# P V products of a head pair in one visit, the relative bias as one float32r pass, and another set of stream delays

## The chip, the cores and the metric

The kernel runs on one core of one Trainium2 chip. The metric is the device time of one execution in microseconds; the time given is the median of several runs. The engines are TensorE (PE, with its weight loads as PEld), VectorE (DVE), ScalarE (ACT), GpSimd (POOL) and SyncE (SP, which here only issues DMAs).

## The reference

One decoder layer on 512 tokens of width 1024. Eight attention heads and eight Gated DeltaNet heads, all of width 64, share one input projection and one output projection; RMSNorms stand ahead of and behind both halves, and a squared-ReLU MLP of width 4096 follows.

```python
h = rms_norm(x, pre_mix_norm[l])
proj = einsum('bsd,dc->bsc', h, w_in[l])
att_q, att_k, att_v, gdn_qkv, gdn_z, gdn_a, gdn_b = split(proj, split_points, axis=-1)
o_att = moba_attention(att_q, att_k, att_v, rel_bias)
o_gdn = gated_deltanet(gdn_qkv, gdn_z, gdn_a, gdn_b, conv_w[l], A_log[l], dt_bias[l], gdn_norm_w[l])
mix = einsum('bsc,cd->bsd', concatenate([o_att, o_gdn], axis=-1), w_out[l])
x = x + rms_norm(mix, post_mix_norm[l])
h = rms_norm(x, pre_mlp_norm[l])
m = einsum('bsf,fd->bsd', square(relu(einsum('bsd,df->bsf', h, w_up[l]))), w_down[l])
x = x + rms_norm(m, post_mlp_norm[l])
```

The attention works on blocks of 256 keys and picks three past blocks for each query. With 512 tokens there are two blocks, so it is plain causal attention. Its logits are `q k / 8 + rel_bias[head, bucket(q_pos - k_pos)]` with 32 buckets of distance; then softmax, then the product with `v` (P V below). The DeltaNet part runs over chunks of 64 tokens: a convolution of four taps with SiLU, normalized q and k, the inverse of a unit lower triangular matrix per chunk and head, and a recurrence over eight chunks.

## The kernel before

Large products are made from float32r operands split into a high part `hi` and a remainder `lo`; `mm3` issues the three products hi hi, hi lo and lo hi. ACT rounds to `hi`, and DVE or POOL subtracts to get `lo` (`split`, `load_split`, `ended`). Transposes and small products stay in float32; in the trace a float32 product of 128x64 shape leaves two records.

**Order of TensorE.** TensorE's instructions run in the order in which the Python program emits them. The program is a set of generators (streams) that a small planner, `Weave` (L47), interleaves. It keeps a clock `now` that `mm` (L96) and `transpose` (L100) advance by an assumed duration. A stream yields a delay, or the name of a mark; the planner runs the stream of lowest rank whose time has come. Delays come from the table `WAIT` (L20) by kind; `SINGLE` (L22) overrides the n-th use of a kind, for example `('conv_k', 1)`. `RANK` (L24) gives the order of the streams, `LEAD` (L25) a priority that the other engines' scheduler uses, `START` (L28) some fixed moments of the opening, and `LO_DVE` (L30) the range of weight loads whose `lo` is subtracted on DVE rather than POOL. A delay is thus not a wait on the chip: it decides where in TensorE's queue the next piece of a stream stands. On the chip TensorE waits if the data of its next instruction aren't there. ACT, DVE and POOL run in emission order in the opening (`pre_norm`, `in_order`) and in the scheduler's order afterwards, until the MLP. SP issues DMAs.

**The streams.**

- `projections` (the main stream, rank 5 and last): 24 items of 128 output columns in the sequence of `ORDER` (L29), each 24 matmuls of 512 columns, and the attention's `v` by token. `x0` to `x3` are the q's and `y0` to `y3` the k's of the four pairs of attention heads. `x2` and `x3` wait for the marks `att0` and `att1`, whose buffers they take.
- `take_k`, `take_q`, `take_v`, `take_z`: convolution and so on of each DeltaNet item as it leaves PSUM; `conv_k` is the delay between an item's convolution and the transposes of `kraw`.
- `chunks`, `inverse`, `scan`, `finish_o`: DeltaNet. The inverse is 31 steps of two DVE instructions; the scan's matmuls have 32*32, 64*64 and 128*64 shapes.
- `bias`, `scores`, `values`: the attention. Four pairs of heads, four blocks of 128 tokens.
- `weights_out`, `output`, `weights_up`, `up0`: output projection and the start of the MLP, which runs behind all this in an order of its own.

**PSUM.** Eight banks in three tags: `mm` (2), `g` (3) and `a` (3), by `bank` (L175).

**Bias.** `bias_in` (L197) loads a 33 x 640 table of zeros and ones (`c_hot`, as `hot`) and the 32 x 8 biases with a 33rd row of -1e30 (`rb`), right behind the loads of `x` and of the first weights. `bias` (L651) multiplies them in float32 in two products of 512 and 128 columns and stores the result to DRAM (`d_e`), from which `scores` reads it in a skewed form.

**Scores and values.** For each pair `scores` (L682) makes rows 3, 2, 1 and 0 of the logits, the triangular part alone, and their exponentials; each row sets a mark `row{p}{q}` after the delay `rows`. `values` (L720) transposes the exponentials (`block(k)`: keys of block k, all later queries, into bank tag `a`, copied by ACT into `ph` tiles, of which four stand) and multiplies with `v` (`product(k, P)`: one matmul for each of the two heads, onto one bank `po`, also of tag `a`). The order is

```python
P = block(3)
po = bank("a")
for k in (2, 1, 0):
    yield f"row{p}{k}"
    if k > 0:
        N = block(k)
    yield wait["pv"]
    product(k + 1, P)
    if k == 0:
        N = block(0)
    P = N
```

so the products of blocks 3, 2 and 1 come each after the delay `pv`, and the transposes of block 0 directly behind product 1. Then the mark `turned{p}` lets the next pair's scores begin; the reciprocal sums are transposed into a bank `rb`, ACT copies them to SBUF, and after the delay `pv0` the last product is issued. DVE multiplies `po` with the sums (`mx`), `split` rounds it, and `att{p}` is marked after the delay `att`.

Of the kernel before, what the change touches and what calls it, by code (L numbers as in the profile page):

```python
# [85 lines left out]
def layer(ctx, tc, nc, x, w_in, w_v, w_ab, w_out, w_up, w_down, conv_w, a_log, dt_bias, gdn_norm_w, rel_bias,  # L86
# [633 lines left out]
    def values():  # L720
        for p in range(4):
# [812 lines left out]
```

## Time and profile before

| | us |
|---|---|
| median of 3 runs | 635.08 |
| lowest and highest run | 632.75, 635.93 |
| span of the profiled execution, first to last instruction | 634.2 |

The profile gives the span of the profiled execution; a time of its own is not listed for it. The span is 0.88 us under the median of the runs. Mean granted TensorE clock: 0.998.

Busy time by stage, from the view by windows:

| us from the start | PE | DVE | ACT | POOL | DMA share |
|---|---|---|---|---|---|
| 0 to 20 | 17.47 | 9.55 | 10.61 | 9.20 | 0.66 |
| 120 to 140 | 20.00 | 18.80 | 9.09 | 2.59 | 0.27 |
| 140 to 160 | 19.70 | 18.72 | 8.24 | 0.00 | 0.28 |
| 180 to 200 | 19.75 | 6.06 | 16.38 | 7.72 | 0.17 |
| 240 to 260 | 19.60 | 10.61 | 15.44 | 3.99 | 0.31 |
| 360 to 634 (MLP) | 267.66 of 274 | 222.86 | 164.30 | 40.24 | 0.86 |

How to read it: a row of the views in order of time has the start in us, the time from the start to the end of the group, the engine, the line of the kernel, the operation, `out<-in` by the program's names, the tile shape of TensorE (contraction rows * output rows), the operand and the count of records; idle time ahead of it and what ended that stand in brackets. Matmuls are pipelined and their ends are modelled, so the distance between two starts says more than a duration.

### The profile page before, as it was taken

What the parts mean: (1) busy time and instruction counts of PE and PEld (TensorE: products, weight loads), DVE (VectorE), ACT (ScalarE), POOL (GpSimd) and SP (SyncE); (2) the same over time, 40 slices, a digit from 0 to 9 for tenths busy, and PEclk for the clock granted to TensorE, in tenths of its full rate; (3) what the DMA queues carried; (4) which work ended last, traced back from release to release, by engine and by line L of the source; (5) the groups of instructions that cost most, each with busy time, mean ns of one, the idle gap of its engine ahead of it and who ended that gap; (6) DMA issues with size and microseconds to landing.
All of it is one profiled execution on the core that took longest, in us unless ns stands there. A gap on an engine that the chain in (4) does not pass through costs nothing.

```text
span 634.2 us, 11129 instructions
## 1 busy us (share of the span) xinstructions
PE 622.9 (98%) x4359; PEld 524.1 (83%) x4359; DVE 443.7 (70%) x635; ACT 359.4 (57%) x610; POOL 157.9 (25%) x197
## 2 busy tenths in 40 slices
PE   8999999999999999999999999999999999999995
PEld 6877777877876777688998999999998888888884
DVE  4456667599724464658665678878789888887776
ACT  6366586254387548654225586566765656665661
POOL 4346555500234343004212311111130320000001
PEclk9999999999999999999999999999999999999999
DMA  7222332422731112563488899999999999867503
GB/s 247 78 90 83 84 109 76 128 88 71 186 94 52 36 35 82 188 229 132 162 336 233 159 276 268 228 241 286 270 264 340 310 291 285 270 213 283 198 1 132
DMA packets 60629, 113.16 MB, mean 178 GB/s; under 512 B 15734, under 2 KB 35321, under 8 KB 60194
## 3 DMA queue, kind: packets, MB, share of 16 engines
q1 hardware_dynamic: 42876, 83.09, 37.8%
q0 software_dynamic: 17696, 29.36, 22.2%
q8 instruction: 34, 0.56, 0.3%
q14 instruction: 17, 0.14, 0.1%
q10 hardware_dynamic: 6, 0.00, 0.0%
HBM read 106.65 MB, written 35.15 MB: 224 GB/s over the span
## 4 chain that ended last, share of the span: by engine, by line
PE 91%; DVE 3%; DMA 2%; ACT 2%; POOL 1%; issue 0%; POOLq 0%; DVEq 0%; SPq 0%; ACTq 0%
PE ps_mm L97 46%; PE ps_g L97 26%; PE ps_a L97 16%; PE ps_a L101 2%; PE ps_g L101 1%; DMA wo_raw<-in_w_out 1%; DMA xx<-in_x 1%; DVE conv L412 1%; DMA w_raw<-in_w_in 0%; DVE wo_l L143 0%; POOL w_lo L155 0%; POOL oss L192 0%; DVE hT_l L131 0%; POOL by L192 0%; DVE xs L249 0%
## 5 line engine op out<-in xcount | busy, mean ns | idle before, releaser
L130 ACT CAST wdh<-wd 128x1024 fp32r<-128x1024 f32 x53 | 55.9, 1054 | 51.4 <-PE ps_mm L97 22.6
L131 DVE TENSOR_TENSOR u_l<-w,u_h 128x1024 fp32r<-128x1024 f32 x46 | 56.2, 1224 | 37.3 <-ACT u_h L130 37.1
L131 DVE TENSOR_TENSOR wdl<-wd,wdh 128x1024 fp32r<-128x1024 f32 x53 | 64.9, 1224 | 22.2 <-ACT wdh L130 22.1
L130 ACT CAST u_h<-w 128x1024 fp32r<-128x1024 f32 x46 | 47.9, 1046 | 56.8 <-DVE w L1177 15.6
L97 PE MATMUL ps_mm<-hT_h,w_hi 128*128 128x512 f32 (+1 forms) x192 | 79.4, 413 | 0.0
L97 PE MATMUL ps_mm<-hT_l,w_hi 128*128 128x512 f32 (+1 forms) x192 | 74.6, 388 | 0.3 <-DVE hT_l L131 0.3
L97 PE MATMUL ps_mm<-hT_h,w_lo 128*128 128x512 f32 (+1 forms) x192 | 74.5, 388 | 0.0
L155 POOL TENSOR_TENSOR w_lo<-w_raw,w_hi 128x512 fp32r<-128x512 f32 x40 | 51.8, 1297 | 77.2 <-ACT w_hi L154 67.4
L1210 POOL DMA_DIRECT2D d_T<-in_w_down x32 | 33.0, 1033 | 143.8 <-DMA d_T<-in_w_down 82.4
L154 ACT CAST w_hi<-w_raw 128x512 fp32r<-128x512 f32 x56 | 34.6, 620 | 52.9 <-PE ps_mm L97 17.5
L97 PEld LDWEIGHTS ps_mm<-hT_h,w_hi 128*128 128x128 f32 x192 | 37.1, 193 | 11.3 <-issue 4.8
L97 PE MATMUL ps_mm<-wdh,u_h 128*128 128x512 f32 x116 | 45.2, 390 | 0.0
L97 PE MATMUL ps_mm<-wdl,u_h 128*128 128x512 f32 x116 | 45.1, 389 | 0.0
L97 PE MATMUL ps_mm<-wdh,u_l 128*128 128x512 f32 x116 | 45.1, 389 | 0.0
L97 PEld LDWEIGHTS ps_mm<-hT_h,w_lo 128*128 128x128 f32 x192 | 37.2, 194 | 7.5
L97 PEld LDWEIGHTS ps_mm<-hT_l,w_hi 128*128 128x128 f32 x192 | 37.3, 194 | 6.0 <-DVE hT_l L131 0.6
L412 DVE SCALAR_TENSOR_TENSOR conv<-ps_mm,cw,conv 128x511 f32<-128x511 f32 (+2 forms) x36 | 26.8, 745 | 11.3 <-ACT conv L409 11.0
L131 DVE TENSOR_TENSOR u_l<-f,u_h 128x1024 fp32r<-128x1024 f32 x28 | 34.1, 1217 | 0.0
L708 DVE CUSTOM_DVE_ANT_0 L<-ps_a,E 128x512 f32<-128x512 f32 (+3 forms) x32 | 14.4, 489 | 23.9 <-PE ps_a L97 23.7
L97 PE MATMUL ps_g<-wdh,u_h 128*128 128x512 f32 x80 | 31.1, 389 | 0.0
L97 PE MATMUL ps_g<-wdl,u_h 128*128 128x512 f32 x80 | 31.1, 389 | 0.0
L97 PE MATMUL ps_g<-wdh,u_l 128*128 128x512 f32 x80 | 31.1, 389 | 0.0
(452 smaller groups left out, 1761.3 us busy)
## 6 DMA issues: line engine op xcount, KB each, us to landing
d_T<-in_w_down POOLq DMA_DIRECT2D x48, 512.0 KB, 11.6
wd<-d_T SPq DMA_DIRECT2D x32, 512.0 KB, 6.2
w<-in_w_up SPq DMA_DIRECT2D x28, 512.0 KB, 8.0
wd<-in_w_down SPq DMA_DIRECT2D x24, 512.0 KB, 7.7
w_raw<-in_w_in SPq DMA_DIRECT2D x46, 256.0 KB, 2.7
wo_raw<-in_w_out SPq DMA_DIRECT2D x16, 256.0 KB, 3.4
d_T<-d_T POOLq DMA_DIRECT2D x8, 512.0 KB, 12.7
xx<-in_x SPq DMA_DIRECT2D x4, 512.0 KB, 6.4
```

The costliest lines, as they stand in the source:

```text
L97: nc.tensor.matmul(o, l, r, **kw)
L101: nc.tensor.transpose(o, i, ident[:k, :k])
L130: nc.scalar.copy(hi, src)
L131: tt(lo, src, f32(hi), op=OP.subtract)
L154: nc.scalar.copy(hi, raw)
L155: (sub or tt)(lo, raw, f32(hi), op=OP.subtract)
L412: stt(c[:, s:], p[:, :512 - s], cw[:, ft, j:j + 1], c[:, s:], op0=OP.mult, op1=OP.add)
L708: nc.vector.tensor_tensor_reduce(out=l, in0=s[hh][:, :w], in1=Es[hh][:, w - 1::-1], scale=1.0, scalar=3e38, op0=OP.add, op1=OP.min, accum_ ...
L1210: nc.gpsimd.dma_start(d_T[t][k], block(b, second)[k], accum_op=OP.add, max_dma_last_dim=1024)
```

## The change

Three parts.

1. `values` issues all four `block` transposes of a pair first and all eight P V matmuls (four `product` steps of two) together, after `rb` and the delay `pv0`. `po` is taken only then. The delay `pv` is no longer used. `ph` has eight buffers for four.
2. The bias product is made in float32r: the 33-row table is doubled to 97 rows (rows 0 to 32 and 64 to 96), the biases are split into a rounded part in rows 0 to 32 and the remainder in rows 64 to 96 of `rs`, and one pass multiplies both. New are a memset of `rs`, a copy of the table by POOL that rounds it to float32r, a copy by ACT and a subtraction by DVE; these three are issued at `START[3]`.
3. `WAIT`, `SINGLE`, `RANK`, `LEAD`, `START` and `LO_DVE` have other values, and in `ORDER` `v0` and `v1` change places. `SINGLE` has 147 entries where it had 36; among the new ones are `('pv0', 1): 4.83`, `('rows', 7): 8.76`, `('state', 5): 2.54` and `('scalars', 0): 4.42`, `('conv_k', 1)` stays 5.1 and `('kk_out', 0)` goes from 11.93 to 6.79.

```diff
-WAIT = {'h': 1.7, 'conv_k': 5.5, 'k': 5.19, 'conv_q': 6.15, 'q': 2.1, 'conv_v': 11.0, 'v': 6.02, 'z': 2.87, 'ab': 0.1, 'g': 11.93, 'scalars': 4.76, 'r_in': 0.65, 'r_out': 4.45, 'kk': 2.71, 'kk_out': 14.43, 'gl': 3.13, 'qk': 3.88, 'va': 0.83, 'a': 5.81, 'row': 1.38, 'rows': 5.12, 'pv': 1.54, 'att': 1.17, 'inverse': 1.23, 'merge': 11.0, 'p1': 2.8, 'p2': 1.7, 'w': 2.33, 'vn': 1.0, 'state': 1.21, 'o_in': 3.96, 'o': 3.73, 'wo': 0.97, 'wo_out': 17.6, 'normed3': 7.6, 'normed': 11.21, 'n': 1.7, 'up': 1.9, 'sums': 2.64, 'turned': 0.5, 'pv0': 1.53}
+WAIT = {'h': 0.86, 'conv_k': 5.48, 'k': 6.06, 'conv_q': 5.48, 'q': 2.49, 'conv_v': 11.04, 'v': 3.81, 'z': 2.47, 'ab': 2.97, 'g': 7.94, 'scalars': 6.37, 'r_in': 0.44, 'r_out': 4.15, 'kk': 3.12, 'kk_out': 21.2, 'gl': 5.7, 'qk': 2.04, 'va': 1.87, 'a': 5.44, 'row': 2.47, 'rows': 5.12, 'pv': 1.45, 'att': 3.93, 'inverse': 0.39, 'merge': 9.84, 'p1': 3.55, 'p2': 0.79, 'w': 1.67, 'vn': 1.0, 'state': 2.43, 'o_in': 3.89, 'o': 3.36, 'wo': 3.23, 'wo_out': 26.28, 'normed3': 11.89, 'normed': 13.4, 'n': 2.23, 'up': 0.86, 'sums': 2.41, 'turned': 0.42, 'pv0': 4.1}
...
-RANK = {'chunks': 1, 'inverse': 3, 'scan': 3, 'scores': 5, 'values': 5, 'finish_o': 2, 'take': 4}
-LEAD = {'chunks': 0, 'inverse': 100, 'scan': 100, 'scores': 0, 'values': 100, 'finish_o': 0, 'take': 200, 'take_a': 100}
+RANK = {'chunks': 2, 'inverse': 2, 'scan': 1, 'scores': 4, 'values': 4, 'finish_o': 3, 'take': 4}
+LEAD = {'chunks': 300, 'inverse': 50, 'scan': 200, 'scores': 100, 'values': 0, 'finish_o': 300, 'take': 50, 'take_a': 200}
...
-START = (5.5, 9.7, 18.5, 13.8, 30, 15.0)
-ORDER = "k0 q0 x0 k1 q1 q2 y0 k2 k3 z0 q3 x1 w0 v0 v1 v2 v3 y1 x2 y2 x3 y3 z1 z2 z3"
-LO_DVE = (26, 40)
+START = (6.58, 9.48, 15.98, 12.4, 30.84, 15.19)
+ORDER = "k0 q0 x0 k1 q1 q2 y0 k2 k3 z0 q3 x1 w0 v1 v0 v2 v3 y1 x2 y2 x3 y3 z1 z2 z3"
+LO_DVE = (29, 48)
...
     def bias_in():
-        hot, es = he[:33, :640], he[:8, 640:]
+        hot, es = he[:97, :640], he[:8, 640:]
...
+        rs = at.tile([97, 8], FR, name="rs", bufs=1)
+        nc.vector.memset(f32(rs), 0.0)
...
     def bias():
-        hot, es, rb = rel
+        hot, es, rb, rs = rel
+        hot_r = at.tile([128, 1280], FT, name="L")[:97, :640].bitcast(FR)
+        yield max(0, START[3] - weave.now)
+        nc.gpsimd.tensor_copy(hot_r, hot)
+        nc.scalar.copy(rs[:33], rb)
+        tt(rs[64:97], rb, f32(rs[:33]), op=OP.subtract)
         yield max(0, START[4] - weave.now)
         for a, b in ((0, 512), (512, 640)):
             pe = bank("a")
-            mm(pe[:8, :b - a], rb, hot[:, a:b], start=True, stop=True)
+            mm(pe[:8, :b - a], rs, hot_r[:, a:b], start=True, stop=True)
...
-                    pt = at.tile([128, 512], FT, name="ph", bufs=4)
+                    pt = at.tile([128, 512], FT, name="ph", bufs=8)
...
-            P = block(3)
-            po = bank("a")
+            P = {3: block(3)}
             for k in (2, 1, 0):
                 yield f"row{p}{k}"
-                if k > 0:
-                    N = block(k)
-                yield wait["pv"]
-                product(k + 1, P)
-                if k == 0:
-                    N = block(0)
-                P = N
+                P[k] = block(k)
             mark(f"turned{p}", wait["turned"])
             yield f"sums{p}"
             rb = bank("a")
...
             yield wait["pv0"]
-            product(0, P)
+            po = bank("a")
+            for k in (3, 2, 1, 0):
+                product(k, P[k])
...
-    hot = np.zeros((33, 640), f)
-    hot[bucket, 127 + d] = 1
-    hot[32, :127] = 1
+    hot = np.zeros((97, 640), f)
+    for o in (0, 64):
+        hot[o + bucket, 127 + d] = 1
+        hot[o + 32, :127] = 1
```

More of the change, by code (lines that the diff above doesn't have):

```diff
@@ L22 @@
-SINGLE = {('h', 0): 0.05, ('inverse', 6): 2.02, ('state', 6): 3.71, ('row', 5): 0.98, ('inverse', 18): 0.05, ('inverse', 25): 0.05, ('vn', 7): 0.05, ('pv', 2): 0.1, ('h', 1): 0.05, ('turned', 0): 0.9, ('conv_k', 0): 4.12, ('normed', 0): 10.21, ('wo', 1): 1.97, ('conv_q', 0): 8.0, ('inverse', 16): 1.63, ('state', 1): 1.57, ('row', 6): 0.38, ('conv_v', 1): 8.5, ('conv_q', 2): 7.0, ('conv_k', 1): 5.1, ('o_in', 1): 4.36, ('kk', 2): 2.03, ('h', 2): 0.85, ('rows', 2): 6.66, ('vn', 1): 0.75, ('pv', 4): 2.77, ('inverse', 0): 0.61, ('rows', 0): 5.52, ('pv', 6): 2.0, ('rows', 4): 0.1, ('conv_v', 0): 14.3, ('kk_out', 0): 11.93, ('gl', 0): 5.63, ('inverse', 27): 0.23, ('row', 12): 2.48, ('state', 0): 0.21}
@@ new lines @@
+SINGLE = {('h', 0): 4.85, ('inverse', 6): 2.02, ('state', 6): 3.66, ('row', 5): 0.98, ('inverse', 25): 0.05, ('vn', 7): 0.14, ('pv', 2): 0.1, ('normed', 0): 10.24, ('wo', 1): 0.05, ('conv_q', 0): 8.69, ('inverse', 16): 1.63, ('state', 1): 1.57, ('row', 6): 0.33, ('conv_v', 1): 7.83, ('conv_k', 1): 5.1, ('kk', 2): 2.03, ('vn', 1): 0.75, ('pv', 4): 2.77, ('inverse', 0): 0.93, ('rows', 0): 6.08, ('pv', 6): 2.0, ('rows', 4): 0.22, ('conv_v', 0): 14.23, ('kk_out', 0): 6.79, ('inverse', 27): 0.23, ('row', 12): 2.48, ('state', 0): 0.05, ('vn', 4): 0.05, ('g', 0): 11.27, ('pv0', 3): 5.63, ('n', 1): 2.8, ('row', 9): 4.41, ('inverse', 20): 1.09, ('state', 4): 1.35, ('inverse', 28): 4.43, ('rows', 7): 8.76, ('w', 2): 2.04, ('kk', 0): 2.54, ('normed3', 0): 7.79, ('n', 2): 1.44, ('o_in', 2): 4.99, ('state', 5): 2.54, ('r_in', 3): 1.7, ('w', 3): 2.33, ('scalars', 0): 4.42, ('rows', 5): 4.36, ('row', 3): 4.58, ('n', 0): 5.62, ('z', 3): 0.05, ('inverse', 3): 1.71, ('inverse', 9): 4.8, ('state', 2): 3.37, ('o_in', 1): 1.66, ('ab', 0): 1.85, ('inverse', 12): 1.27, ('va', 0): 0.05, ('o_in', 0): 0.94, ('sums', 0): 1.83, ('r_in', 0): 0.83, ('q', 3): 4.02, ('wo', 9): 2.75, ('rows', 11): 4.94, ('r_in', 2): 0.05, ('up', 1): 2.69, ('k', 0): 6.39, ('row', 13): 2.25, ('inverse', 21): 0.68, ('pv0', 2): 2.33, ('up', 6): 0.71, ('up', 2): 1.8, ('z', 1): 1.9, ('rows', 9): 5.32, ('rows', 6): 4.96, ('row', 15): 2.64, ('row', 1): 1.47, ('a', 0): 4.5, ('att', 2): 0.15, ('wo', 14): 10.37, ('wo', 13): 5.87, ('r_out', 2): 4.4, ('rows', 8): 4.94, ('v', 0): 13.69, ('conv_k', 3): 5.47, ('up', 0): 1.03, ('att', 1): 1.03, ('conv_q', 3): 4.72, ('normed', 1): 13.89, ('rows', 1): 6.91, ('inverse', 2): 0.05, ('wo', 8): 4.61, ('k', 1): 4.72, ('turned', 0): 0.05, ('vn', 3): 1.16, ('q', 2): 4.06, ('pv0', 1): 4.83, ('q', 0): 2.14, ('o', 1): 0.14, ('o', 3): 4.07, ('vn', 2): 3.12, ('k', 3): 5.87, ('up', 5): 2.84, ('wo_out', 0): 19.88, ('inverse', 10): 0.9, ('merge', 0): 10.94, ('v', 2): 12.67, ('w', 0): 1.68, ('inverse', 19): 1.66, ('pv0', 0): 4.87, ('conv_q', 1): 4.99, ('wo', 2): 1.79, ('z', 0): 0.05, ('inverse', 24): 1.39, ('a', 3): 5.23, ('wo', 11): 3.51, ('rows', 3): 6.28, ('inverse', 14): 0.15, ('att', 0): 3.37, ('row', 10): 2.37, ('conv_k', 0): 5.11, ('v', 3): 14.1, ('normed', 2): 12.25, ('z', 2): 0.05, ('row', 2): 2.64, ('kk', 1): 3.86, ('wo', 12): 3.29, ('r_in', 1): 0.05, ('turned', 3): 0.69, ('q', 1): 2.97, ('att', 3): 4.49, ('turned', 2): 0.25, ('v', 1): 8.52, ('up', 3): 0.37, ('wo', 4): 3.7, ('gl', 0): 5.22, ('kk', 3): 4.48, ('vn', 6): 1.14, ('sums', 1): 1.59, ('inverse', 4): 0.32, ('row', 8): 1.29, ('k', 2): 5.51, ('h', 1): 2.26, ('row', 14): 2.55, ('n', 3): 1.82, ('inverse', 1): 0.05, ('wo', 5): 6.26, ('p2', 0): 0.05, ('r_out', 1): 5.83}
@@ L203, in bias_in @@
         nc.sync.dma_start(rb[:32], rel_bias)
-        return hot, es, rb
+        rs = at.tile([97, 8], FR, name="rs", bufs=1)
+        nc.vector.memset(f32(rs), 0.0)
+        return hot, es, rb, rs
     def pre_norm(ahead):
```

## The prediction

> **What bounds the kernel now.** I read the page first: engine shares, the 40 slices, the chain that ended last.
>
> ```profile
> span 634.2 us, 11129 instructions
> ...
> PE 622.9 (98%) x4359; PEld 524.1 (83%) x4359; DVE 443.7 (70%) x635; ACT 359.4 (57%) x610; POOL 157.9 (25%) x197
> ...
> PE   8999999999999999999999999999999999999995
> ...
> PE 91%; DVE 3%; DMA 2%; ACT 2%; POOL 1%; issue 0%; POOLq 0%; DVEq 0%; SPq 0%; ACTq 0%
> ```
>
> TensorE is busy in every slice and is 91% of the chain. So a microsecond is won only if TensorE issues less, or if one of its own gaps closes; what other engines gain is worth nothing by itself. A busy PE isn't a full PE, however, since ends are modelled. I therefore go by starts, and ask next for the waits of PE in the first 280 us, the part that the change touches:
>
> ```profile
> PE ps_g L101 <- DVE kraw L416: 1.0, 1, 1.0
> ...
> PE ps_a L101 <- ACT ph L736: 0.3, 1, 0.3
> PE ps_a L97 <- ACT t L762: 0.2, 1, 0.2
> ```
>
> Little is left to win there: the largest wait behind the opening is 1.0 us, and the next that matter are on tiles of the bank tag `a`. The remainder has to come from how matmuls of different shapes follow each other. The order in time shows that:
>
> ```profile
> 132.28 0.39 PE L97 MATMUL ps_mm<-hT_h,w_lo 128*128 128x512 f32 x1
> 132.51 0.82 PE L101 MATMUL ps_a<-ident,L 128*128 128x128 f32 x6
> 133.09 0.48 PE L97 MATMUL ps_mm<-hT_h,w_hi 128*128 128x512 f32 x1
> 133.40 0.40 PE L97 MATMUL ps_mm<-hT_l,w_hi 128*128 128x512 f32 x1
> 133.63 0.39 PE L97 MATMUL ps_mm<-hT_h,w_lo 128*128 128x512 f32 x1
> ...
> 138.25 0.40 PE L97 MATMUL ps_mm<-hT_h,w_lo 128*128 128x512 f32 x1
> 138.57 0.65 PE L97 MATMUL ps_a<-ph,V 128*64 128x256 f32 x4
> 139.16 0.50 PE L97 MATMUL ps_mm<-hT_h,w_hi 128*128 128x512 f32 x1
> 139.50 0.40 PE L97 MATMUL ps_mm<-hT_l,w_hi 128*128 128x512 f32 x1
> ...
> 140.06 0.87 PE L97 MATMUL ps_a<-ph,V 128*64 128x384 f32 x4
> 140.86 1.09 PE L101 MATMUL ps_a<-ident,L 128*128 128x128 f32 x8
> 142.24 0.66 PE L101 MATMUL ps_a<-ident,R 128*128 128x128 f32 x4 [0.29 <-ACT ph L736]
> ```
>
> The first number is the start. A projection matmul of 512 columns starts 0.23 us after the one before (133.40 to 133.63). The visit of six transposes costs nothing beyond its matmuls: 132.28 to 133.40 is 1.12, less two projection steps (0.46) leaves 0.66, or 0.11 a transpose. A P V visit is dearer than its work: it starts 0.32 after the last projection (138.25 to 138.57), 0.09 over a step, and the second projection behind it comes 0.34 after the first (139.16 to 139.50), 0.11 over.
>
> **Part 1, the eight products in one visit.** How much is lost inside a run shows where two visits happened to stand together, in a later stretch:
>
> ```profile
> 181.35 0.40 PE L97 MATMUL ps_mm<-hT_h,w_lo 128*128 128x512 f32 x1
> ...
> 187.58 1.30 PE L97 MATMUL ps_a<-ph,V 128*64 128x256 f32 x8
> 188.81 1.09 PE L101 MATMUL ps_a<-ident,L 128*128 128x128 f32 x8
> ...
> 191.04 0.50 PE L97 MATMUL ps_a<-pt 64*128 64x512 f32 x1
> 191.79 0.96 PE L97 MATMUL ps_a<-pt 64*128 64x512 f32 x5 [0.25 <-ACT t L762]
> 192.68 0.69 PE L97 MATMUL ps_g<-UT,kB 64*64 64x64 f32 x32
> ...
> 195.03 0.50 PE L97 MATMUL ps_mm<-hT_h,w_hi 128*128 128x512 f32 x1
> ```
>
> The products over 256 and 384 columns took 0.59 (138.57 to 139.16) and 0.80 (140.06 to 140.86) apart, 1.39 together, and 1.23 as one run (187.58 to 188.81). So a visit that vanishes between projections gives 0.09 + 0.11 + 0.16 = 0.36 us. How many vanish?
>
> ```profile
> L97 PE MATMUL ps_a<-ph,V x64: 272/458/643, 135.3 to 260.8; 128*64 128x128 f32 x16, 128*64 128x256 f32 x16, 128*64 128x384 f32 x16, 128*64 128x512 f32 x16
> ```
>
> ```profile
> 203.94 1.09 PE L97 MATMUL ps_g<-S,LWQ 128*64 128x128 f32 x16
> 204.86 0.39 PE L97 MATMUL ps_a<-ph,V 128*64 128x128 f32 x4
> ```
>
> 64 records, four to a product step, are 16 steps, four for each of four pairs; afterwards there are four visits. Twelve go, but not each is worth 0.36. Pairs 0 and 3 stand among projections and give three each, 6 x 0.36. Pairs 1 and 2 lie in the scan: two steps are already one run (187.58), others ride behind matmuls of the same 128*64 shape (204.86) or stand between two tiled shapes, where a switch remains. I count 1.5 for these six. That is 7.5 x 0.36 = 2.7 us. Bounds: 1.4 (seven, with entry and exit alone, 0.20) and 4.0 (eleven at 0.36).
>
> [...]
>
> The last block of transposes, which used to follow a product directly, gets a visit of its own; transposes among projections are free, as shown. The number of `ph` copies on ACT is unchanged; eight buffers hold a pair's six tiles without waiting for products. The products now come behind `rb` and `pv0`, so `att` of each pair is later; the cover is the projections and the scan (see the slow rival).
>
> **Part 2, a bank comes free.** `po` used to hold one of the three `a` banks from a pair's first block on. Two places pay for it. Eight transposes from 140.86 need 0.88 at 0.11 and would let `R` start near 141.8; it started at 142.24, waiting for the `ph` copy: 0.44 lost. At 191.04 one score matmul went, and its five companions came 0.75 later, behind the copy that frees the bank of `rb`; the five needed 0.89 (to 192.68) as if nothing had been saved. With `po` taken only for the visit, the three banks serve blocks, `rb` and scores. Together 1.2; I take 0.9, since `po` now asks for a bank itself, right after `rb`. Bounds: 0 and 1.2.
>
> **Part 3, the bias.**
>
> ```profile
> 33.40 0.39 PE L97 MATMUL ps_mm<-hT_h,w_lo 128*128 128x512 f32 x1
> 33.72 1.24 PE L97 MATMUL ps_a<-L,rb 33*8 33x512 f32 x4
> 34.89 0.66 PE L101 MATMUL ps_g<-ident,kraw 128*128 128x128 f32 x4
> ```
>
> Two float32 products leave four records and 1.17 us. One float32r pass steps 512 columns in 0.23 and so 128 in 0.06: 0.29. Gain 0.88; I take 0.8 for the exit that remains. Bounds 0.5 and 0.9: no 97*8 form is in the trace. Its preparation:
>
> ```profile
> 15.78 1.29 POOL L155 TENSOR_TENSOR w<-nb,w 128x512 fp32r<-128x512 f32 x1
> ...
> 17.97 1.24 POOL L382 CAST picks<-cload 128x512 fp32r<-128x512 f32 x2 [0.90 <-DMA cload<-in_c_sel]
> ```
>
> ```profile
> L<-in_c_hot SPq DMA_DIRECT2D x1, 82.5 KB
> ```
>
> POOL casts 512 columns in 0.62, so 640 in 0.78. By START the cast is issued behind the weight subtraction of 15.78 and ahead of `picks`, where POOL stood idle 0.90. It fits; uncovered it would push later weight subtractions by 0.8. The constant grows from 33 to 97 rows, some 160 KB more on SP's queue, behind all of `x` and the first weights. The small copies on ACT and DVE, and LO_DVE, which hands some weight subtractions from POOL to DVE and a few back, lie on engines 57%, 70% and 25% busy. All this I take at zero, 0.8 lost at most (the cast bare).
>
> **Part 4, the delays.** They change no instruction, only the order of TensorE's queue and priorities elsewhere. From the trace I can't sum them; I take 0. They can win the 1.0 wait on `kraw` (its delay `('conv_k', 1)` stays 5.1, so I don't count on it) and lose as the rivals say.
>
> **Sum.** -2.7 - 0.9 - 0.8 = -4.4 us: a span of 629.8. The median of the three runs is 635.08, 0.9 over the profiled span, and I carry that difference: **630.7**. With the bounds of the three parts (1.9 to 6.1 us) the forecast's own range is 629.0 to 633.2.
>
> **Rivals.**
> *The gaps close too.* Longer waits ahead of transposes and projections also remove the 1.0 at `kraw` and some smaller ones, and more tiled visits fall together, two or three at 0.36: 1.7 in all, 629.0. For: most delays grow. Against: that one doesn't.
>
> *Visits come apart.* Between 182 and 246 us tiled shapes follow each other (187.58 to 192.68 holds no projection). If the new order sets projections between eight of these, 8 x 0.36 = 2.9 is given back: 633.6, no change that can be told. The same holds if pairs 1 and 2 give nothing and the banks' waits move elsewhere.
>
> *TensorE runs dry before pair 3's projections.* The projection of `x3` needs `att1`. Between 181.35 and 195.03 none was issued: the stream was blocked, and scan, scores and values filled the time. The change delays `att1` further: `('rows', 7)` is 8.76 where 5.12 stood, and `('pv0', 1)` 4.83 where 1.53 stood, 6.9 us in all, while no filler is added. If all of it is bare, the loss is 6.9. A cold start then comes on top, seen in the opening:
>
> ```profile
> 12.97 0.41 PE L97 MATMUL ps_mm<-hT_h,w_hi 128*128 128x256 f32 x1
> 13.19 0.41 PE L97 MATMUL ps_mm<-hT_l,w_hi 128*128 128x256 f32 x1
> ...
> 17.24 0.40 PE L97 MATMUL ps_mm<-hT_h,w_lo 128*128 128x256 f32 x1
> ```
>
> ```profile
> 26.11 0.28 PE L97 MATMUL ps_mm<-hT_l,w_hi 128*128 128x256 f32 x1
> 26.23 0.28 PE L97 MATMUL ps_mm<-hT_h,w_lo 128*128 128x256 f32 x1
> ```
>
> 256 columns step 0.22 until 17.24 and 0.12 later, so 4.3 us of slow steps lose 1.9. Together 8.8: 639.5, slower. It decides from a bare gap of 7.6 us, cold steps included (4.4 + 0.5% of 635). Against: a delay is only an order; TensorE starts the next instruction as soon as its data are there. [...]
>
> **How the numbers follow.** Forecast 0.48, gaps close 0.17, visits come apart or a bare gap of some 3 to 5 us (to 636) 0.24, dry 0.11. About 0.5%, 3.2 us, is what a measurement of this kernel can tell from no change: faster is below 631.9, slower above 638.3. Of the forecast's chance 0.05 lies above 631.9, near its weak end. So faster 0.43 + 0.17 = 0.60, same 0.05 + 0.24 = 0.29, slower 0.11. The range reaches from 627.0 (gaps closed, and Part 1 near its upper bound) to 637.0.
>
> **What would show it.** Four runs of 16 `ph`,V records in place of 16 steps; the bias below 0.4 us; no wait for `ph` L736 or `t` L762 on PE; about the same count of projections between 182 and 195. Wrong, if PE shows a new wait over 2 us on `mx`, `UT`, `kB` or `hT`, or if P V run length per product doesn't shrink.

## The result and the profile after

| | before | after |
|---|---|---|
| median of 6 runs each, us | 634.05 | 641.97 |
| lowest and highest | 632.75, 635.93 | 641.05, 642.42 |
| span of the profiled execution | 634.2 | 640.6 |

The ratio is 1.0124, with a 95% interval from 1.0105 to 1.0144: slower by 7.9 us, and outside the range of 627 to 637. First the page of the changed kernel: span, busy time of TensorE, its granted clock in 40 slices, and the chain by engine.

```profile
span 640.6 us, 11125 instructions
...
PE 619.0 (97%) x4357; PEld 523.0 (82%) x4357; DVE 451.0 (70%) x642; ACT 360.0 (56%) x611; POOL 154.4 (24%) x193
...
PEclk9799999999999999999999999999999999999998
...
PE 87%; DMA 4%; DVE 4%; ACT 2%; POOL 1%; issue 1%; SPq 0%; POOLq 0%; DVEq 0%; ACTq 0%
```

TensorE is busy 3.9 us less than before (619.0 against 622.9), and yet the span is 6.4 us longer. Busy time counts slow steps too, so the 3.9 isn't the saving itself, but the loss must lie in gaps and slow steps. DMA grew on the chain from 2% to 4%, and the second slice has a 7, a clock between 0.7 and 0.8. Which gaps, the waits of PE between 8 and 280 us say (total, times, longest, in us; the seven largest):

```profile
PE ps_g L97 <- ACT hT_h L130: 4.7, 1, 4.7
PE ps_mm L97 <- DVE conv L414: 1.7, 1, 1.7
PE ps_g L101 <- DVE ot L926: 1.7, 1, 1.7
PE ps_g L101 <- DVE kraw L418: 1.3, 1, 1.3
PE ps_g L97 <- ACT mg_h L130: 0.9, 1, 0.9
PE ps_mm L97 <- DVE hT_l L131: 0.8, 1, 0.8
PE ps_g L97 <- DVE mg_l L131: 0.7, 1, 0.7
```

Before, the largest behind the opening was 1.0 on `kraw`. The waits on `ph` and on `t` (L762), 0.3 and 0.2 before, are gone. In order of time, on PE:

```profile
24.03 0.64 PE L97 MATMUL ps_g<-hT_h,abw 128*32 128x512 f32 x1 [4.68 <-ACT hT_h L130]
...
26.35 0.63 PE L97 MATMUL ps_g<-hT_h,abw 128*32 128x512 f32 x1
26.78 0.63 PE L97 MATMUL ps_g<-hT_l,abw 128*32 128x512 f32 x1
...
29.87 0.40 PE L97 MATMUL ps_g<-hT_l,abw 128*32 128x512 f32 x1
30.11 0.39 PE L97 MATMUL ps_g<-hT_h,abw 128*32 128x512 f32 x1
...
38.17 0.46 PE L97 MATMUL ps_a<-L,rs 97*8 97x512 f32 x2
38.47 0.45 PE L97 MATMUL ps_mm<-hT_h,w_hi 128*128 128x512 f32 x1
...
144.02 2.37 PE L97 MATMUL ps_a<-ph,V 128*64 128x128 f32 x16
146.33 0.50 PE L97 MATMUL ps_mm<-hT_h,w_hi 128*128 128x512 f32 x1
...
194.55 2.37 PE L97 MATMUL ps_a<-ph,V 128*64 128x128 f32 x16
...
223.19 2.37 PE L97 MATMUL ps_a<-ph,V 128*64 128x128 f32 x16
...
260.46 2.37 PE L97 MATMUL ps_a<-ph,V 128*64 128x128 f32 x16
```

The parts are there. The bias takes 0.30 us (38.17 to 38.47) in place of 1.17. There are four runs of 16 `ph`,V records, the first 2.31 us (144.02 to 146.33). But at 24 us TensorE stands still for 4.68 us, and afterwards a matmul of 512 columns steps 0.43 us (26.35 to 26.78) in place of 0.23, until some 29.4 us. The view by windows has the granted clock for it (0.72, the third figure from the end):

```profile
20.00:32.00 12.00, 7.57 (x29) 3.94 (x30) 3.29 (x8) 3.72 (x9) 2.66 (x7) 0.72 0.34 109
```

What ACT waited for is seen in its own order of time:

```profile
21.50 0.20 ACT L658 CAST rs<-rb 33x8 fp32r<-33x8 f32 x1 [7.27 <-DMA rb<-in_rel_bias]
22.04 0.21 ACT L535 ACTIVATE ea<-alg 128x8 f32<-128x8 f32 x1 [0.35 <-DMA alg<-in_a_log]
22.22 0.30 ACT L130 CAST abw<-abr 128x128 fp32r<-128x128 f32 x1
22.42 1.07 ACT L130 CAST hT_h<-ps_g 128x512 fp32r<-128x512 f32 x2
```

In before the second of these stands without a wait:

```profile
15.31 0.21 ACT L533 ACTIVATE ea<-alg 128x8 f32<-128x8 f32 x1
```

ACT runs in emission order here, so the cast of `hT_h`, whose input TensorE had delivered by 18.7 us, stands behind a copy of 33x8 that waits 7.27 us for a load of 1 KB. That load comes right behind the table `c_hot` on SP's queue. The packet records of the trace say why (packets of 2560 B are the rows of the table; times in us from the span's start):

```
kernel        rows  packets  first start  last end  median ns from start to start
before          33       33        10.69     12.34     37.5
after           97       97        11.10     20.77     99.0
e1_rows128     128      128        10.50     12.57     11.0
e5_before97     97       97        11.10     20.75     99.0
```

A packet takes about 102 ns (median) with 97 or 128 rows, 113 in before. 97 rows go one after the other, a start every 99 ns, 9.7 us in all. 128 rows overlap: packets of some 102 ns, 128 of them in 2.1 us, are about six at a time on the mean. With the 33 rows of before at most 7 overlap. What makes 97 rows go singly isn't shown.

To see where the rest was lost, take the start of the same matmul in each kernel minus that in before (us; `proj` numbers the matmuls with `hT` as an operand, 736 in each kernel, from 0):

```
                  proj 48  proj 192  proj 432  proj 528  proj 600  first wo  first wu  first T2h
after               +1.94     +5.04     +3.75     +4.32     +4.76     +3.44     +5.55      +6.39
e1_rows128          -0.07     -0.16     -1.45     -1.08     -0.64     -1.77     +0.00      +0.83
e4_part1            -0.07     -0.52     -0.53     -1.76     -1.05     +8.99    +11.34     +13.27
e8_bias             -1.95     -3.70     +1.55     +1.54     +1.54     +4.00     +4.02      +4.02
e11_bias_q1         -1.32     -2.69     -1.02     -1.02     -1.02     -0.64     -0.62      -0.62
e9_p3_before        -2.28     -2.61     -2.61     -4.17     -3.54     +6.33     +7.47      +7.47
e13_small_visits    -0.16     -0.09     -1.38     -1.13     -0.70    +11.43    +11.26     +12.07
e7_o_in             -3.38     -3.29     -4.58     -4.33     -3.89     -4.80     -2.31      -1.49
e10_ma_first        -2.88     -2.31     -3.60     -3.31     -2.88     -6.03     -3.52      -2.69
```

A first column below zero is no gain of the kernel: in the opening the granted clock comes to full speed at 17.5 us in the profile of before, at 17.7 in that of `e1_rows128` and at 10.3 in that of `e7_o_in` (matmuls of 256 columns step 0.22 us up to 17.24, 0.21 up to 17.6, and 0.12 from 11.46 on), although the last two have the same code up to there. So rows are read from the first column on, and the medians, over several executions, decide. The profiled execution of before was moreover a slow one: the times of its executions lie 1.85 to 1.97 us above their spans in the later runs, which makes some 636.1 us of its span of 634.2, more than any of the six above.

### The profile page after: what moved, and what is told of

Same layout as the page of the kernel before. It is cut to its first block, busy times and chain, and to the rows that moved or that the text cites. A ratio compares the mean times of both kernels' runs of the same rounds, so it can differ in the third digit from the quotient of the medians.

```text
span 640.6 us, 11125 instructions
## 1 busy us (share of the span) xinstructions
PE 619.0 (97%) x4357; PEld 523.0 (82%) x4357; DVE 451.0 (70%) x642; ACT 360.0 (56%) x611; POOL 154.4 (24%) x193
## 4 chain that ended last, share of the span: by engine, by line
PE 87%; DMA 4%; DVE 4%; ACT 2%; POOL 1%; issue 1%; SPq 0%; POOLq 0%; DVEq 0%; ACTq 0%
PE ps_mm L97 43%; PE ps_g L97 25%; PE ps_a L97 16%; PE ps_a L101 2%; DMA alg<-in_a_log 2%; DMA wo_raw<-in_w_out 1%; PE ps_g L101 1%; DMA w_raw<-in_w_in 1%; DMA xx<-in_x 1%; DVE xs L1034 1%; DVE hT_l L131 0%; DVE conv L414 0%; POOL g L1255 0%; ACT wo_h L142 0%; DVE wo_l L143 0%
## 5 line engine op out<-in xcount | busy, mean ns | idle before, releaser
L97 PE MATMUL ps_mm<-hT_h,w_hi 128*128 128x512 f32 (+1 forms) x192 | 77.5, 404 | 2.0 <-DVE conv L414 1.7
L155 POOL TENSOR_TENSOR w_lo<-w_raw,w_hi 128x512 fp32r<-128x512 f32 x35 | 45.2, 1294 | 37.2 <-ACT w_hi L154 33.9
L130 ACT CAST u_h<-f 128x1024 fp32r<-128x1024 f32 x28 | 29.3, 1046 | 0.0
## 6 DMA issues: line engine op xcount, KB each, us to landing
d_T<-d_T POOLq DMA_DIRECT2D x8, 512.0 KB, 11.3
```

The source lines that it names most:

```text
L97: nc.tensor.matmul(o, l, r, **kw)
L130: nc.scalar.copy(hi, src)
L155: (sub or tt)(lo, raw, f32(hi), op=OP.subtract)
```

## The experiments

"Before" beside each is the median of the runs of before on the same chip.

**The table's rows.** The first kernel pads the table to 128 rows of which 97 are used, the second loads 97 rows into before.

```diff
# e1_rows128, against after
-        nc.sync.dma_start(hot, c_hot)
+        nc.sync.dma_start(he[:128, :640], c_hot)
-    hot = np.zeros((97, 640), f)
+    hot = np.zeros((128, 640), f)
# e5_before97, against before
-        nc.sync.dma_start(hot, c_hot)
+        nc.sync.dma_start(he[:97, :640], c_hot)
-    hot = np.zeros((33, 640), f)
+    hot = np.zeros((97, 640), f)
# e2_late_cast, against after
-        yield max(0, START[3] - weave.now)
+        yield "h3"
```

> The changed kernel, with the table of the bias padded from 97 to 128 rows of zeros, and nothing else. Theory A (the load of 97 rows goes as 97 packets one behind the other, and everything behind it on SP's queue lands late): the table lands by 13 us where it took until 21, TensorE's wait of 4.7 us for hT_h at 24 us and the slow steps after it go, and the time falls by 5 to 7 us to 635 to 637. Rival B (the new casts on the ordered engines are what holds them, whatever the load): 642 stays. Rival C (the new delays place the streams badly): 642 stays, within 1.

> The kernel before, with a table of 97 rows loaded in place of 33; its product still uses rows 0 to 32 and nothing new is computed. Theory A: the loads behind the table come late and ACT stands before the exponential of a_log, 5 to 7 us over the kernel before: 639 to 641. Rivals B and C: no change, 634.

> The changed kernel with its 97 rows, and the three preparing instructions of the bias issued only after the fourth tile of x is rounded, so that they hold no cast of hT. Theory A: the small loads behind the table (a_log, w_ab) still land at about 22 us, and ACT, in order, stands before the exponential of a_log; 640 to 642. Rival B: the wait for hT_h goes, 635 to 637. Rival C: 642.

| kernel | median us | before | ratio, 95% |
|---|---|---|---|
| `e1_rows128` | 637.10 | 634.64 | 1.0041, 1.0020 to 1.0061 |
| `e5_before97` | 639.63 | 634.64 | 1.0084, 1.0054 to 1.0113 |
| `e2_late_cast` | 641.46 | 634.64 | 1.0113, 1.0084 to 1.0143 |

The larger load was the faster one: 128 rows take 4.9 us off the changed kernel, and 97 rows in before, where nobody uses them, cost 5.0. Moving the casts changes nothing that can be told: ACT then stands 7.26 us before the load of `a_log`, and TensorE 3.4 before `hT_h`. So the row count is the cause of this part, not the place of the casts. `e1_rows128` came out 0.1 us above the range expected of it. Without it the change is still 0.4% slower, and not faster as forecast.

**The delays.** All tables of before in the changed kernel with 128 rows; and only the `state` delays of the scan.

```diff
# e3_old_delays, against e1_rows128
-WAIT, SINGLE, RANK, LEAD, START, ORDER, LO_DVE of after
+WAIT, SINGLE, RANK, LEAD, START, ORDER, LO_DVE of before
# e6_state, against e1_rows128: 'state' alone
-WAIT 'state': 2.43; SINGLE ('state', 0): 0.05, 1: 1.57, 2: 3.37, 4: 1.35, 5: 2.54, 6: 3.66
+WAIT 'state': 1.21; SINGLE ('state', 0): 0.21, 1: 1.57, 6: 3.71
```

> The 128 rows, one visit per pair and the float32r bias, with all delays, ranks, priorities and the sequence of the kernel before. If the terms of the prediction's sum are right (2.7 visits, 0.9 bank, 0.8 bias), it runs 4.4 us under the kernel before: 629 to 631. Rival C says that the new delays lose several us, so that this one lies 3 to 6 us under e1_rows128; if the new delays are worth something, it lies above e1_rows128.

> e1_rows128 (all of the change, table of 128 rows) with the delays of the kind state as they were in the kernel before. Theory D (the longer state delays end the scan so late that the normalization of the last tile stands bare behind the last projection): the wait for ot (1.8 us) and those for mg_h and mg_l (1.3) go, 633 to 635. Rival: these waits have another cause, or as much appears elsewhere: 636.5 or more.

`e3_old_delays` took 648.53 us (1.0222, 1.0180 to 1.0264), `e6_state` 639.44 (before 635.08; 1.0068, 1.0045 to 1.0091). The new delays aren't what loses: they are worth 11.4 us to the new structure. With those of `state` alone put back, some 2 us are lost (2.3 by the medians, 1.9 when each is counted from its own before; the two intervals overlap), and the wait on `ot` gives way to one of 3.6 us on `om`. So theory D fell: the longer `state` delays don't make that wait.

**Each part alone, in before.** Part 1 is the one visit with eight `ph` buffers; the bias comes with a table of 128 rows.

```diff
# e4_part1, against before: values() of after
+            P = {3: block(3)}
...
+            po = bank("a")
+            for k in (3, 2, 1, 0):
+                product(k, P[k])
# e8_bias, against before: bias_in(), bias() and c_hot of after, 128 rows
# e11_bias_q1, against e8_bias: one SINGLE entry
+('q', 1): 3.5
```

> The kernel before with one visit per pair (and eight ph buffers) alone: old bias, old delays. If the prediction's terms hold by themselves (2.7 visits, 0.9 bank): 631. If the loss of e3_old_delays (648.5) comes from the one visit standing among delays that were made for four: 644 to 649.

> The kernel before with the float32r bias alone, table of 128 rows: old values, old delays. By the prediction's term 0.8 us less than the kernel before, 633.5 to 634.2, with a bias visit of 0.3 us where it took 1.2. If the loss of e3_old_delays comes from the bias: 640 or more.

> Before with only the float32r bias (637.57 us), and one group of four q transposes put behind six more projection matmuls (1.4 us), with nothing else moved on TensorE. Theory A (the 2.5 us lost there are the 1.89 us wait on sqt at 64.1 us and the 6.8 us of half clock that follow it): wait below 0.6, no slow window at 65 us; 633 to 634.7, the 0.6 to 0.9 us of the bias pass then show. Rival B (the cast or the small copies of the bias cost the time elsewhere): 636.5 to 638.

| kernel | median us | before | ratio, 95% |
|---|---|---|---|
| `e4_part1` | 647.25 | 635.08 | 1.0188, 1.0158 to 1.0217 |
| `e8_bias` | 637.57 | 635.08 | 1.0041, 1.0020 to 1.0062 |
| `e11_bias_q1` | 635.42 | 633.88 | 1.0024, 1.0007 to 1.0041 |

Each part loses under the delays of before, and neither of the two bias runs lies in a range that was expected of it. For the bias the order of time on PE of the profiled execution of `e8_bias` shows how little it takes:

```profile
61.87 0.39 PE L97 MATMUL ps_mm<-hT_h,w_lo 128*128 128x512 f32 x1
64.14 0.66 PE L101 MATMUL ps_g<-ident,sqt 128*128 128x128 f32 x4 [1.89 <-ACT sqt L453]
...
69.34 0.63 PE L97 MATMUL ps_mm<-hT_h,w_lo 128*128 128x512 f32 x1
69.77 0.63 PE L97 MATMUL ps_mm<-hT_h,w_hi 128*128 128x512 f32 x1
...
72.49 0.40 PE L97 MATMUL ps_mm<-hT_l,w_hi 128*128 128x512 f32 x1
72.73 0.39 PE L97 MATMUL ps_mm<-hT_h,w_lo 128*128 128x512 f32 x1
```

TensorE reaches these transposes ahead of ACT's `sqt`, waits 1.89 us, and then steps 0.43 in place of 0.23 from 65.3 to 72.1 (6.83 us in the clock records of the trace). With the transposes 1.4 us later, `e11_bias_q1`, the wait is 0.5 and no slow stretch follows; the first matmul on `T2h` falls from +5.97 to +0.70, both counted from projection 48. Of these 5.3 us, 3.6 lie between projections 192 and 432, where the wait and the slow stretch are; the rest is mostly another wait of `e8_bias` that `e11_bias_q1` hasn't, 1.5 on `S` at 230 us. The medians fall less, from 2.5 over before to 1.5, with intervals that overlap, since the profiled execution of `e8_bias` was its slowest (640.90, median 637.57). So the wait and the clock behind it explain that execution; what they cost in the median isn't shown.

The pass's gain does show: between projections 48 and 192 `e11_bias_q1` wins 1.4 us (-1.32 to -2.69), 0.87 by the pass and 0.4 by a shorter wait on `kraw`. It is lost again by 432; the two waits that stand there, 0.5 on `sqt` and 0.4 on `ssq`, account for half of it, and the other half stays open. Counted from projection 48 it is then 0.7 behind before at the first matmul on `T2h`. Another 0.8 is no cost of the pass: from the last matmul to the end `e8_bias` and `e11_bias_q1` take 7.4 us, each of the other 15 profiles 6.5 to 6.6, since their last store lands 6.3 us behind that matmul in place of 5.5. In these two a packet of 8192 B, of the queue that the profile names `q14 instruction`, runs beside the store for 0.86 us (it starts 4.5 us behind the last matmul). In before such a packet comes only behind the store, and `e3_old_delays`, which has the bias too, has none there. What places this packet stays open. The 0.7 and the 0.8 together are the 1.5 of the medians.

**Where the one visit loses.** My theory after the first runs was that pair 3's small visits, which stood between the last projections, had covered the way of `z3` from PSUM to the output. `e9_p3_before` gives pair 3 its four visits back in `e4_part1`; `e13_small_visits` undoes Part 1 in `e1_rows128` under the new delays.

```diff
# e9_p3_before, against e4_part1, for p == 3 alone
+                if p == 3:
+                    yield wait["pv"]
+                    product(k + 1, P[k + 1])
# e13_small_visits, against e1_rows128: values() of before, four ph buffers
```

> Pairs 0, 1 and 2 keep the one visit of the kernel before with only Part 1 (647.25 us, 12.2 over before); pair 3 alone gets its four product visits back, so that TensorE's order from pair 3 on is that of before. Theory A (pair 3's small visits between the last projections were the cover for the evacuation of z3, and the clock halves behind the bare waits that come instead): the waits on om (3.1) and mg_h and the two windows of slow clock near 252 and 269 us go, 12 us with them; 633 to 636. Rival B (the bunched visits of the other pairs do not fit the old delays): at most pair 3's own share of the visits changes, 644 to 648.

> The changed kernel with 128 rows (637.1 us) with Part 1 alone undone: the products in four visits per pair and four buffers, but all the new delays. Theory A (the one visit by itself is worth some 0.36 us for each vanished visit, and its loss comes only where the order leaves the scan and the output without cover): small visits under the delays made for one visit lose at least the 2.7 us of the forecast, 639.5 to 643, and pair 3's small visits do not repair the end of the scan, whose delays stay. Rival B (the one visit costs more than it saves whatever the delays): 632 to 636.

`e9_p3_before` took 646.25 us (before 633.88; 1.0205, 1.0172 to 1.0238), so that theory fell: pair 3 alone isn't the place. `e13_small_visits` took 646.05 (before 634.38; 1.0177, 1.0141 to 1.0213): under the new delays the small visits lose by even more than I gave them. With the bias in float32r and 128 rows the four combinations are, in us:

| | delays of before | delays of after |
|---|---|---|
| small visits | 637.57 | 646.05 |
| one visit | 648.53 | 637.10 |

The four ran on two chips, whose befores differ by at most 0.7. Neither visits nor delays have a price of their own; each of these two sets of delays fits one structure, and the wrong pair costs 8.5 to 11.4 us. What these are, the waits of PE between 180 and 280 us show. In before, all of them:

```profile
PE ps_g L101 <- DVE om L933: 0.4, 1, 0.4
PE ps_a L97 <- ACT t L762: 0.2, 1, 0.2
```

In `e9_p3_before`, the largest:

```profile
PE ps_g L97 <- ACT vn L891: 3.0, 2, 2.2
PE ps_mm L97 <- ACT mg_h L130: 1.9, 1, 1.9
PE ps_g L97 <- DVE S L902: 1.5, 2, 0.9
PE ps_g L101 <- DVE om L937: 1.1, 1, 1.1
PE ps_a L97 <- ACT ph L736: 1.1, 1, 1.1
```

The sum of this view's rows is 0.6 us in before, 9.5 in `e9_p3_before`, 10.4 in `e4_part1`, 8.1 in `e13_small_visits` and 3.3 in `e1_rows128`. Waits and slow clock account for the whole loss: from projection 48 to the first matmul on `T2h`, `e4_part1` takes 13.3 us longer than before; its waits of 0.15 and more sum to 12.6 in place of 1.9, and 10.24 us at half clock cost up to 5.1 more, so that the rest is up to 2.5 us shorter. The names tell the place: `vn` and `S` are steps of the scan, a chain of TensorE, ACT and DVE in turn, and `om` and `mg_h` its way to the output. One such step in the order of time of `e9_p3_before`:

```profile
246.04 1.09 PE L97 MATMUL ps_g<-S,LWQ 128*64 128x128 f32 x16
246.97 0.39 PE L97 MATMUL ps_a<-ph,V 128*64 128x128 f32 x4
247.29 0.33 PE L97 MATMUL ps_g<-vn,AT 64*64 64x64 f32 x2
249.82 1.58 PE L97 MATMUL ps_g<-vn,AT 64*64 64x64 f32 x30 [2.21 <-ACT vn L891]
```

`vn` is ACT's copy of what the first row makes. Only four P V records are left to stand between; TensorE waits 2.21 us, and its clock is at half from 250.3 for 3.41 us. But missing cover isn't all of it. ACT's order in `e9_p3_before` has two steps ahead of `vn`, the first of which waits for a load of `w_out`:

```profile
248.02 0.62 ACT L142 CAST wo_h<-wo_raw 128x512 fp32r<-128x512 f32 x1 [0.91 <-DMA wo_raw<-in_w_out]
248.54 0.62 ACT L480 ACTIVATE t<-zs 128x512 f32<-128x512 f32 x1
249.19 0.58 ACT L891 COPY vn<-ps_g 64x512 f32<-64x512 f32 x1
```

So the copy starts 2.1 us after its input is made (246.04 + 1.09). In before, the last step of the scan stands 5.7 us earlier, and ACT copies at once:

```profile
240.35 1.09 PE L97 MATMUL ps_g<-S,LWQ 128*64 128x128 f32 x16
241.50 0.58 ACT L887 COPY vn<-ps_g 64x512 f32<-64x512 f32 x1
```

The same cast, waiting 1.26 us for its load, stands ahead of `mg_h` in `e4_part1`. Under the old delays, then, the bunched visits put the scan's end among the casts of `w_out`, and TensorE has too little else to do there. How much of the loss is missing cover and how much is ACT's order and the loads isn't separated by any run.

**The end of the scan under the new delays.** `e7_o_in` moves the last four transposes of `ot` behind 21 products of the output; `e10_ma_first` moreover takes the attention's halves first there, in the products and in the loads of `w_out`; `e14_before_ma` does the latter in before.

```diff
# e7_o_in, against e1_rows128: one SINGLE entry
+('o_in', 3): 46.0
# e10_ma_first, against e7_o_in (e14_before_ma, against before)
-            for z in (1, 0):
-                if (b, z) == (1, 0):
+            for i in (1, 0):
+                z = 1 - i
+                if (b, i) == (1, 0):
...
-            for k in (4, 5, 6, 7, 0, 1, 2):
+            for k in (0, 1, 2, 4, 5, 6, 7):
```

> e1_rows128 with one delay changed, so that the four transposes of the last tile (ot) stand behind 21 matmuls of the output projection and not ahead of them; TensorE's order is otherwise the same. Theory D: the wait of 1.8 us for ot goes, 635.0 to 635.6. If the matmuls behind have to wait for something of their own (the rounded tiles or weights), it only changes its name: 636.5 to 637.5.

> The kernel with 128 rows and the last four transposes later (636.2 us); in addition the output's products take the halves of the attention (k 0 to 2) ahead of those of the scan (k 4 to 7), and w_out's rows are loaded in that order. Nine matmuls of 0.23 = 2.07 us, which do not need z3, then stand between pair 3's products and the first one that does. Theory A (one visit took the cover from z3's evacuation): the 2.1 wait on mg_h L130 goes or falls below 0.5, and the 0.7 and 0.8 behind it; 632.7 to 634.2, faster than before. Rival B (ACT or the loads of w_out bound that place): the wait moves to wo_h casts or ma_h, 635.5 to 637.

> The kernel before, with only the output's products taken attention halves first and w_out loaded in that order. It has no wait there beyond 0.4 on om and 0.1 on mg. Theory A (the 2.7 us that this order won in the changed kernel were cover that the one visit had taken away): no change that can be told, 633.4 to 634.4. Rival B (the order is a gain of its own in any kernel): 631 to 632.5.

| kernel | median us | before | ratio, 95% |
|---|---|---|---|
| `e7_o_in` | 636.18 | 635.08 | 1.0017, 0.9999 to 1.0035 |
| `e10_ma_first` | 633.49 | 633.88 | 0.9993, 0.9976 to 1.0009 |
| `e14_before_ma` | 634.39 | 634.38 | 0.9993, 0.9975 to 1.0012 |

In `e7_o_in` the wait on `ot` is gone and another stands in its place, since `z3` is only then on its way:

```profile
252.20 2.37 PE L97 MATMUL ps_a<-ph,V 128*64 128x128 f32 x16
256.63 0.50 PE L97 MATMUL ps_mm<-wo_h,mg_h 128*128 128x512 f32 x1 [2.05 <-ACT mg_h L130]
```

In `e10_ma_first` nine products that need no `z3` stand there (255.40 to 257.58):

```profile
253.09 2.37 PE L97 MATMUL ps_a<-ph,V 128*64 128x128 f32 x16
255.40 0.50 PE L97 MATMUL ps_mm<-wo_h,ma_h 128*128 128x512 f32 x1
...
257.58 0.40 PE L97 MATMUL ps_mm<-wo_h,mg_h 128*128 128x512 f32 x1
```

By the medians 2.7 us are won, but 1.2 of it is the other chip's before (635.08 and 633.88). Counted from each one's own before it is 1.5, with intervals that overlap; from projection 48 to the first matmul on `T2h` the two traces say 1.7. The same edit wins nothing that can be told in before. ACT's cast of `mg_h` ends 4.4 us after the start of the 16 products in `e7_o_in` and 4.2 in `e10_ma_first`, so the late data came hardly sooner for the new order of the loads: what changed is what TensorE had to do meanwhile. So this was cover that the changed kernel lacked. Both edits together are clear of the noise (1.0041, 1.0020 to 1.0061 in `e1_rows128`; 0.9993, 0.9976 to 1.0009 here), and with them the change stands level with before.

**The next two waits.** `e12_two_waits` gives cover to those on `conv` (1.7) and `kraw` (1.5) of `e10_ma_first`, `e15_kraw` to `kraw` alone.

```diff
# e12_two_waits, against e10_ma_first
-None if LO_DVE[0] <= n < LO_DVE[1] else nc.gpsimd.tensor_tensor
+None if LO_DVE[0] <= n < LO_DVE[1] and n not in (32, 33) else nc.gpsimd.tensor_tensor
-('conv_k', 1): 5.1
+('conv_k', 1): 5.9
# e15_kraw, against e10_ma_first: the conv_k entry alone
```

> The kernel with the attention's halves first in the output (633.5 us, its profile 631.5), with two more of the after kernel's new waits given cover: two weight subtractions (n 32 and 33) go from DVE to POOL, which stands idle there, so that the conv steps behind them end some 1.3 us earlier (wait on conv L414 1.7 to about 0.4), and the group of four kraw transposes goes behind three more projection matmuls, 0.68 us (wait on kraw 1.45 to about 0.8). Theory A (what is missing from the forecast gain are new waits of this kind, each taken off the path at its length): 631.2 to 632.0, faster than before by 0.3 to 0.4%. Rival B (the gain is eaten by the next wait on the same engines): 633 to 634.

> The kernel with the attention's halves first in the output (633.49 us), and of the two edits tried together only the one on kraw: its four transposes behind three more projection matmuls; the weight subtractions stay on DVE. Theory A (a bare wait of TensorE is worth its length when a matmul can stand ahead of it, and POOL's subtraction beside DVE was what spoilt the pair of edits): kraw's wait 1.45 to about 0.8, conv's stays 1.7; 632.6 to 633.0 against 633.9 to 634.4 of before. Rival B (the next wait takes it all): 633.5 to 634.7.

`e12_two_waits` took 634.72 us (before 634.38; 1.0005, 0.9989 to 1.0022), `e15_kraw` 633.43 (before 634.29; 0.9985, 0.9969 to 1.0000). In both profiles `kraw`'s wait falls, to 0.3 and 0.2, but the median of `e15_kraw` is that of `e10_ma_first`; a gain of 0.7 isn't to be told among executions that lie between 632.1 and 635.9. `e15_kraw` is the best of all, 0.86 under before, with an interval that reaches 1: not shown to be faster. In `e12_two_waits` the wait on `conv` grew from 1.7 to 2.3, where 0.4 was expected. DVE's order of time there:

```profile
147.94 0.34 DVE L784 TENSOR_TENSOR pr<-inv 128x175 f32<-128x175 f32 x1
148.31 1.31 DVE L785 TENSOR_TENSOR inv<-inv,pr 128x175 f32<-128x175 f32 x1
...
150.25 0.74 DVE L414 SCALAR_TENSOR_TENSOR conv<-ps_mm,cw,conv 128x511 f32<-128x511 f32 x1
```

and POOL's, with one of the two subtractions that were given to it:

```profile
147.23 2.20 POOL L155 TENSOR_TENSOR w_lo<-w_raw,w_hi 128x512 fp32r<-128x512 f32 x1 [15.64 <-DVE vt L418]
```

The two instructions overlap. POOL's takes 2.20 us in place of 1.29, DVE's 1.31 where its neighbour of the same size took 0.34. The subtraction, 0.69 us when DVE makes it, left DVE's queue, but the DVE step beside it took 0.97 longer. That this is what held `conv` is read from the rows; no run took the two subtractions alone.

## Why the prediction was wrong

**Part 1, as a visit: right.** The term was 0.36 us for each vanished visit. The 16 records take 2.31 us in one run, where the four products apart held 0.37, 0.58, 0.80 and 1.01 in before (from the start to the next group's, at 250.96, 254.22, 255.71 and 222.69), 2.76 in all. That is 0.15 for each of three vanished visits (the prediction had 0.16), and its entry and exit of 0.09 and 0.11 come on top. Up to 265 us before has 49 visits of smaller tile shapes among the 128*128 matmuls, the changed kernel 41: 8 fewer, where the prediction counted 7.5. In `e4_part1` pair 0 gives 1.23 between projections 432 and 528 (-0.53 to -1.76), where three visits at 0.36 are 1.08 and Part 2 had a share; 0.7 of it is lost again by projection 600.

**Part 2: right in kind under the new delays.** The waits on `ph` and `t` are gone. Under those of before a wait of 1.0 to 1.1 on `ph` stands in `e4_part1` and `e9_p3_before`, so the free bank alone doesn't do it. The upper bound of 1.2 was too large: the 0.75 to the second score matmul holds an ordinary step of some 0.18 (0.89 for five). The 0.9 was not measured alone.

**Part 3, the pass: right.** 0.87 for a term of 0.8.

**Part 3, its preparation: the first step that failed.** It was taken at zero, "0.8 lost at most (the cast bare)". Given its data, the cast does what the prediction said: 0.72 us at 16.74 in `e1_rows128`, right behind the weight subtraction. In the changed kernel it waits 5.46 us for the table. I counted the "some 160 KB more on SP's queue" as bytes, and asked neither how the packets of 97 rows would follow each other nor who stands in order behind that load: `rb`, `alg` and `abr` on SP, then ACT's casts, then TensorE. Measured: 4.9 of the 11.3 us that lie between 630.7 and 641.97.

**Part 4, the delays at zero: the second step that failed.** "They can win the 1.0 wait" and "lose as the rivals say", but the sum took the delays as independent of Part 1. They aren't (the four combinations above). The sentence on Part 1, "the cover is the projections and the scan", has the same error: the scan can't be counted as cover, since it has waits of its own, 2.3 on `vn` and 1.5 on `S` in `e4_part1`.

By the medians `e1_rows128` is 6.4 us above the forecast, and 6.9 when the forecast's -4.4 is counted from the before beside it (2.5 + 4.4). What the new delays leave bare there are 1.7 on `conv` and 3.3 between 180 and 280 us; in all, from projection 48 to the first matmul on `T2h`, its waits sum to 6.5 us where before has 1.9. That stretch is 0.9 longer than before, so the waits cost 4.5 and the three parts saved 3.6, where 4.4 was forecast: within their bounds, and 0.8 short. Waits and shortfall make 5.3 of the 6.9. The remaining 1.6 is about as much as the profiled execution of before lies above before's median (some 636.1 against 634.64); where it lost that isn't shown. Of the waits only those on `ot`, `mg_h` and `kraw` were taken away, and of these only the pair `ot` and `mg_h` gave a gain that can be told (637.10 to 633.49).

**The rivals.** "TensorE runs dry" had the kind of loss, a bare wait and slow steps behind it, at 639.5, but the wrong place and cause: between 180 and 255 us no wait of PE in the changed kernel is over 0.2, so `att1` left no hole. It came at 24 us, from a load. "The gaps close too" was wrong: `kraw` waits 1.3, not 0. "Visits come apart" didn't happen: between 182 and 246 us there are 21 visits of smaller tile shapes before and 19 after.

**What to look for.** The signs of the three parts came: four runs of 16, a bias of 0.30 us, no wait on `ph` or `t`, shorter runs per product. The count of projections between 182 and 195 us didn't stay the same (0 before, 12 after). The sign of being wrong came too, a "new wait over 2 us" on an `hT` tile, but by luck: it stands in the opening, behind a load that the prediction took at zero.

## What to carry to other kernels

When a constant grows, look at its row count and at what is queued behind its load in order, not only at its bytes: here 128 rows were 7.6 us shorter on the wire than 97 (2.1 us from the first packet to the last in `e1_rows128`, 9.7 in the changed kernel). Where an order was fitted to many small visits, refit it with the change that bunches them, never one without the other, and look at which chains of other engines the new order leaves bare. Where TensorE is the bound, put matmuls that need none of the late data into a bare wait: nine of them, put first in the output, won back some 1.6 us.

## What the hardware showed

**Half clock with short waits.** Behind the opening, TensorE's clock stood at half with a wait of 4.68 us in the changed kernel (it ends at 24.03; the granted clock is 0.50 from 22.66 to 29.49 and 1.00 from there to 40), with one of 2.21 in `e9_p3_before` (ends at 249.82; half clock from 250.3 for 3.41) and with one of only 1.89 in `e8_bias` (ends at 64.14; from 65.3 for 6.83). Waits of 2.31 (`e12_two_waits`, ends at 153.54) and 2.05 (`e7_o_in`, ends at 256.63) had none, so the length alone doesn't decide; what else does isn't shown. In the profile of `e8_bias` the wait cost nearly three times its length, by an estimate from its steps (0.43 in place of 0.23): 1.89, and half of 6.83 behind it.

**DVE and POOL beside each other.** In `e12_two_waits` two subtractions that overlapped on the two engines both took longer than their like (above): DVE's 1.31 for 0.34, POOL's 2.20 for 1.29. Two other DVE steps beside the same POOL subtraction did not, 0.69 (at 147.34) and 0.34 (at 147.94). Which overlaps lengthen a step, and by what, isn't shown.
